# Strassen-Winograd products for the first value group of a SwiGLU layer, two of them placed before the second half's norm, and some sums of normed tiles on GpSimd

## The chip, the cores and the metric

One core of one Trainium2 chip. The metric is the device time of one execution in microseconds. Three timed runs of the kernel before gave a median of 2363.04 us (2362.53 to 2363.37).

## The reference

A two-layer trunk on a sequence of 1024 tokens, model width 1024, float32. Layer 0 mixes tokens with softmax attention with a forgetting gate, layer 1 with gated linear attention; each mixer is followed by a SwiGLU feed-forward of hidden width 2816. What matters here is the second half of each layer:

```python
h = modulate(rms_norm(x, norm2_g[i]), sh2, sc2)
x = x + g2[:, None, :] * swiglu(h, ffn_w_in[i], ffn_w_out[i])

def swiglu(h, w_in, w_out):
    gate, up = jnp.split(h @ w_in, 2, axis=-1)
    return (jax.nn.silu(gate) * up) @ w_out
```

## The kernel before, in words

**Number format.** Every float32 operand of a matmul is split into a high part (a cast on ScalarE) and a low part (a subtraction on VectorE or GpSimd), and a product is three matmuls: high by high, high by low, low by high (`mm3`, L305 to L307). Activations are kept transposed, so that a tile is 128 features by 512 tokens. `split_t` (L1516 and L1517 without a shift, L1519 and L1520 with one) splits a tile of activations, `split` (L174, L175) a block of weights.

**Two by two blocks.** The input product of the feed-forward is cut in two by two blocks. The normed input h has four blocks of four tiles each: B11 and B21 hold the first 512 tokens (features 0 to 511 and 512 to 1023), B12 and B22 the second 512. The weights come in groups of 256 output columns: group 0 of the gate, group 0 of the values, group 1 of the gate, and so on (`GROUPS`). A group has four weight blocks A11, A12, A21, A22 (first index: which 128 output columns; second: which 512 features) and four results C11, C12, C21, C22 (columns by token halves).

**Two ways to compute a group.** From the third group on, the loop `for X in gs[2:]` uses the Strassen-Winograd scheme: seven products of a block of four tiles, 12 matmuls each, instead of eight. The sums of weights (`op_sums`, L918 to L920, and `make_s4`, L930) are on GpSimd; the sums of activations are T1 = B12 - B11, T2 = B22 - T1, T3 = B22 - B12 and T4 = B21 - T2, made once per layer and kept as split tiles. The results are put together by additions on VectorE from PSUM (`add`, L1637). The first two groups, gate 0 and value 0, are computed by `plain_tile` instead: eight tiles of 24 matmuls, each over all eight tiles of one half of the tokens. A gate tile ends in a SiLU on ScalarE (L1667), a value tile in a multiplication on VectorE from PSUM (L1669).

**The stage that is changed.** The norm of the first half of the tokens comes early. The gate tiles (0, 0, 0) and (0, 1, 0), written as kind, column block, token half, run on it, and into the second of them are placed the sums over the partitions, the root (L714, L715) and the broadcast of the second half's norm (`rms_spread`, L727, into a PSUM tile called rb). Then `second_half` makes the second half: `normed` (L1512) multiplies the input with rb, `split_t` gives B12 and B22, and for each k the first sum is subtracted on GpSimd (L1701) and split into T1, and the second on VectorE (L1703) and split into T2. The six other plain tiles follow: value (1, 0, 0) on the first half, gate (0, 0, 1) and (0, 1, 1) on the second, and values (1, 0, 1), (1, 1, 1), (1, 1, 0). T3 (L1713) and T4 (L1718) are made behind them. T3 lies in the memory of B12 and T4 in that of the normed tiles y12 and y22, so they wait until those have been read.

**What sets the order.** The program's text gives the dependencies; a planner of the framework decides at compile time, from estimated durations, in which order each engine gets its instructions, and where an instruction of higher priority would not be ready it takes another one that is. At run time every engine works through its list in order. `tc.issue_after(ins)` and `behind_all()` add an order without a wait: the instructions of the block stand behind a given one on their engine. Weight blocks come through `feed.next()`, which keeps `feed.depth` of them in flight; the split blocks go through a ring of six slots, the raw ones through a ring of six views, and the DMA of a raw block is issued when its view has been read. `pin` is a ring of PSUM banks, eight of them in this stage. `tick()` in `prod` lets stores of finished hidden tiles go out after a number of products.

Of the kernel before, what the change touches and what calls it, by code (L numbers as in the profile page):

```python
# [53 lines left out]
def trunk(ctx, tc, x, c, ada_w, ada_b, norm1_g, norm2_g, ffn_w_in, ffn_w_out,  # L54
# [200 lines left out]
    @contextmanager  # L255
    def behind_all():

        bb = nc.cur_bb.bb.instructions
        n = len(bb)
        yield  # L260
        for i in bb[n:]:
            for e, at in split_after.items():
                if i.engine == ENG[e]:
                    tc.add_manual_dep(i, at.name, mybir.DependencyInfo(
                        mybir.DependencyClass.NoSync, mybir.DependencyReason.DATA), reason="order")
# [170 lines left out]
    def last_of(e):  # L436
        return next(i for i in reversed(nc.cur_bb.bb.instructions) if i.engine == ENG[e])
# [321 lines left out]
    class SumSq:  # L759
# [9 lines left out]
        def sums(self, psr, upto=None):  # L769

            if not self.done:
                self.sp = psr([P, self.n], F32, "sp")
            upto = len(self.roots) if upto is None else upto
            for i in range(self.done, upto):
                for t in range(self.n):
                    nc.tensor.matmul(self.sp[:, t:t + 1], self.roots[i][:, psl(t)], ones, start=i == 0 and t == 0,
                                     stop=i == len(self.roots) - 1 and t == self.n - 1)
                if i < len(self.roots) - 1:
                    self.ahead = last_ins()
            self.done = upto  # L780
# [122 lines left out]
    def op_block(l, gr, ab, *after):  # L903

        t = op_tile([depth(gr), P], f"o{l}{gr[0]}{gr[1]}{ab[0]}{ab[-1]}")
        split(t[:, 0], t[:, 1], raws[gr][ab])
        for a in after:
            op_raw(l, *a)
        return as_pair(t)
# [17 lines left out]
    def make_s4(gr):  # L927

        r = raws[gr]
        nc.gpsimd.tensor_sub(r[A12], r[A12], r[A11])  # L930
# [8 lines left out]
    def op_a12(l, gr):  # L939
        w = op_block(l, gr, A12)  # L940
        make_s4(gr)
        return w

    def op_out(l, k0, kc, m0, i):
        mw = 512 // kc
        raw = raw_view(0).rearrange("p (k m) -> p k m", k=kc)
        nc.sync.dma_start(raw, ffn_w_out[l, psl(k0, kc), m0:m0 + mw].rearrange("(k p) m -> p k m", p=P))
        t = op_tile([kc, mw], f"oo{l}{k0}{m0}")
        nc.scalar.copy(t[:, 0], raw)
        (nc.gpsimd if i == 2 else nc.vector).tensor_sub(t[:, 1], raw, t[:, 0].bitcast(F32))  # L950
        return as_pair(t)
# [59 lines left out]
    def ffn_loads(l):  # L1011

        blk = lambda gr, ab, *after: (op_block, l, gr, ab, *after)
        sums = lambda gr, *after: (op_sums, l, gr, *after)
        outs = lambda k0, kc, n: [(op_out, l, k0, kc, m0, i) for i in range(n) for m0 in range(0, D, 512 // kc)]
        g, u = GROUPS[:2]
        four = (A11, A21, A22, A12)
        r = [(op_first, l, g, A11, (g, four), (u, (A11, A12))), blk(g, A12), blk(g, A21), blk(g, A22, (u, (A21, A22)))]
        gs = GROUPS[1:] + OGROUPS
        for a, n in zip(gs, gs[1:] + [None]):  # L1020
            first, then = ((n, four[:2]),), ((n, four[2:]),)
            if n is None:
                first = then = ()
            if a == u:
                r += [blk(a, A11), blk(a, A12, *first), blk(a, A21), blk(a, A22, *then)]
                continue
            r += [blk(a, A11), sums(a, *first)]
            if a[0] < 2:
                r += [blk(a, A11), (op_a12, l, a), blk(a, A21, *then), blk(a, A22), blk(a, A12)]
            else:  # L1030
                r += [(op_s2, l, a), blk(a, A21, *then), blk(a, A12), blk(a, A22), blk(a, "s")]
        return r + outs(NFH - 4, 4, 2 + l)
# [440 lines left out]
    def ffn(l, oh, xs, slots, nm, mid, norm_end, each=None, blocks=None):  # L1473
# [40 lines left out]
        def split_t(t, y, shift=None):  # L1514
            if shift is None:
                nc.scalar.copy(hi(t), y)  # L1516
                nc.vector.tensor_sub(lo(t), y, hi(t).bitcast(F32))  # L1517
            else:
                nc.scalar.activation(hi(t), y, AF.Identity, bias=shift)  # L1519
                nc.vector.scalar_tensor_tensor(lo(t), y, shift, hi(t).bitcast(F32), op0=ALU.add, op1=ALU.subtract)  # L1520
# [24 lines left out]
        def gate_view(i, key):  # L1545

            if i % 2:
                return xs[key[0]][:, hsl(key[1])]
            if key[0] not in sgt:
                sgt[key[0]] = Views(sg[key[0]:key[0] + 1], 2, [HALF], f"sg{l}{key[0]}").v  # L1550
            return sgt[key[0]][key[1]]
# [33 lines left out]
        def hid_done(i, key):  # L1585

            v = {nm_: gate_view(i, k_) for k_, nm_ in BN.items()}
            nm_ = BN[key]
            if (nm_, i) in hid_d:
                defer(1, lambda: hid_out(nm_, i, v[nm_]))  # L1590
            got[i] = got.get(i, 0) + 1
            if i >= NST or got[i] < 4:
                return

            def t13():
                nc.gpsimd.tensor_sub(v["B11"], v["B12"], v["B11"])
                nc.gpsimd.tensor_sub(v["B12"], v["B22"], v["B12"])
                hid_out("T3", i, v["B12"])

            def t2():  # L1600
                hid_out("T1", i, v["B11"])
                nc.gpsimd.tensor_sub(v["B22"], v["B22"], v["B11"])

            def t4():
                hid_out("T2", i, v["B22"])
                nc.gpsimd.tensor_sub(v["B21"], v["B22"], v["B21"])
                hid_out("T4", i, v["B21"])
            defer(2, t13)
            defer(3, t2)
            defer(4, t4)  # L1610
# [36 lines left out]
        def plain_tile(kind, m, hf, after=(), steps=()):  # L1647
            wg = wgs[kind]
            ps = pin([P, HALF], F32, f"p{l}")
            for k in range(8):  # L1650
                if wg[m][k // 4] is None:
                    wg[m][k // 4] = feed.next()
                    feed.depth = 1
                w = wg[m][k // 4]
                t = (b["B12"] + b["B22"])[k] if hf else (B11 + B21)[k]
                with ExitStack() as es:
                    for ins in after:
                        es.enter_context(tc.issue_after(ins))
                    mm3(ps, w.hi[:, k % 4, :], w.lo[:, k % 4, :], hi(t), lo(t), k == 0, k == 7)
                if k in dict(steps):  # L1660
                    at = last_ins()
                    with tc.issue_after(at):
                        dict(steps)[k]()
                    after = (last_of("P"),)
            d = gate_view(0, (m, hf))
            if kind == 0:
                nc.scalar.activation(d, ps, AF.Silu)  # L1667
                return
            nc.vector.tensor_mul(d, d, ps)  # L1669
            hid_done(0, (m, hf))  # L1670

        def spread():
            r1.append(rms_spread(r1[0], f"{l}11", psr))
# [15 lines left out]
        def second_half(rb):  # L1689
            y = y12 + y22  # L1690
            lows = []
            for k in range(8 + 6):
                if k < 8:
                    with tc.issue_after(lows[k - 6]) if k >= 6 else ExitStack():
                        normed(y[k], k, 1, rb)
                k -= 6 - 1
                if 0 <= k < 8:
                    split_t((B12 + B22)[k], y[k], sh(k))
                    lows.append(last_of("D"))
            for k in range(4):  # L1700
                nc.gpsimd.tensor_sub(y11[k], y12[k], y11[k])  # L1701
                split_t(T1[k], y11[k])
                nc.vector.tensor_sub(y11[k], y22[k], y11[k])  # L1703
                split_t(T2[k], y11[k], sh(k + 4))

        second_half(r1[1])
        pin.q.extend(psr.q)
        for kind, m, hf in ((1, 0, 0), (0, 0, 1), (0, 1, 1), (1, 0, 1), (1, 1, 1), (1, 1, 0)):
            plain_tile(kind, m, hf, () if m or hf else (rb_ins[-1],))
        block("T3", H_SL[4:8])  # L1710
        T3 = b["T3"]
        for k in range(4):
            nc.vector.tensor_sub(y12[k], y22[k], y12[k])  # L1713
            split_t(T3[k], y12[k], ds[:, k:k + 1])
        block("T4", slots["to"])
        T4 = b["T4"]
        for k in range(4):
            nc.vector.tensor_sub(y21[k], y21[k], y11[k])  # L1718
            split_t(T4[k], y21[k])
        mid()  # L1720
        bk = list(pin.q)
        pin, pj = Ring(psp, bk[:5]), Ring(psp, bk[5:])
# [200 lines left out]
    def mid(*js):  # L1923
        v = Views(slots["hid"], 2, [HALF], f"ad{js[0]}").v
        ada1_queue(js, v[0][:, 0:256], v[1:4])
        ada1.at -= 20.0
# [553 lines left out]
```

## Time and profile before

| | |
|---|---|
| Median of three runs | 2363.04 us |
| The profiled execution | 2362.25 us |
| Its span, first to last instruction | 2360.5 us |
| Mean granted TensorE clock | 0.994 |
| TensorE busy | 2339.7 us (99%) |
| VectorE busy | 1791.0 us (76%) |
| ScalarE busy | 1122.5 us (48%) |
| GpSimd busy | 1101.5 us (47%) |

All views are of one profiled execution. In a timeline the first number of a row is the start in microseconds from the span's start, the second how long the row's instructions took from the first start to the last end, then engine, line, operation, output and inputs by name, and how many instructions were merged ("x4"). In brackets stands how long the engine was idle before the row and what ended that. PE is TensorE, DVE VectorE, ACT ScalarE, POOL GpSimd, SP the engine that issues the DMAs. The reported duration of one instruction overlaps with the next one's, so that the cost of one in a row of many is read from start to start.

### The profile page before, as it was taken

The page shows a single profiled execution, that of the slowest core. Times are in us where ns is not written, and L with a number is a line of the kernel's source. Part 1 is how long each engine was busy: PE and PEld are TensorE (multiplying, and loading weights), DVE is VectorE, ACT ScalarE, POOL GpSimd, SP SyncE. Part 2 cuts the span into 40 slices and gives each one's busy share as a digit, 9 for nine tenths or more (in the row PEclk, how much of TensorE's full clock was granted, in tenths as well). Part 3 has the DMA queues.
Part 4 walks back from the last instruction along what each step waited for, and adds up shares of the span by engine and source line. Part 5 has one row for each costly group of instructions (what it writes and reads, how often), then busy time and mean ns, then how long its engine had stood idle before and what let it go on. Part 6 is the DMA issues. An engine that isn't in the chain of part 4 may idle for free. (4 is left out here: it accounts for less than half of the span.)

```text
span 2360.5 us, 35758 instructions
## 1 busy us (share of the span) xinstructions
PE 2339.7 (99%) x12208; PEld 1992.7 (84%) x12208; DVE 1791.0 (76%) x2996; ACT 1122.5 (48%) x2186; POOL 1101.5 (47%) x993
## 2 busy tenths in 40 slices
PE   8999999999999999999999999999999999999999
PEld 7888888888888888888888898898888888888888
DVE  6578787886688888885788765668787777876787
ACT  6556566575453343345324644444453433345326
POOL 1334444533355666653363531345446665643262
PEclk8999999999999999999999999999999999999999
DMA  8423333332435545457665543554434544457664
GB/s 265 145 79 113 105 121 95 121 126 99 134 100 173 189 161 170 159 185 259 225 224 170 147 130 93 148 180 169 143 114 163 165 152 147 157 197 259 227 198 150
DMA packets 348719, 375.00 MB, mean 159 GB/s; under 512 B 25500, under 2 KB 286776, under 8 KB 348536
## 3 DMA queue, kind: packets, MB, share of 16 engines
q1 hardware_dynamic: 348536, 372.72, 48.2%
q8 instruction: 96, 1.57, 0.3%
q14 instruction: 87, 0.71, 0.1%
HBM read 275.56 MB, written 97.06 MB: 158 GB/s over the span
## 5 line engine op out<-in xcount | busy, mean ns | idle before, releaser
L175 DVE TENSOR_TENSOR o_s<-xv_s,o_s 128x512 fp32r<-128x512 f32 (+1 forms) x376 | 322.4, 862 | 54.5 <-ACT o_s L174 52.9
L174 ACT CAST o_s<-xv_s 128x512 fp32r<-128x512 f32 (+1 forms) x376 | 216.9, 587 | 290.5 <-PE p_b L307 239.1
L307 PE MATMUL p_b<-B,o_s 128*128 128x512 f32 x608 | 236.0, 389 | 0.0
L305 PE MATMUL p_b<-B,o_s 128*128 128x512 f32 x608 | 235.6, 390 | 0.4 <-DVE x L1637 0.4
L306 PE MATMUL p_b<-B,o_s 128*128 128x512 f32 x608 | 235.9, 389 | 0.0
L918 POOL TENSOR_TENSOR ex_s<-xv_s,xv_s 128x512 f32<-128x512 f32 (+1 forms) x64 | 90.5, 1414 | 285.1 <-DMA xv_s<-in_ffn_w_in_dram 118.8
L1272 POOL TENSOR_SCALAR lp_s<-lp_s,st 128x128 f32<-128x128 f32 (+7 forms) x128 | 98.1, 770 | 246.3 <-DVE st L1271 230.7
L305 PE MATMUL p_b<-T,o_s 128*128 128x512 f32 x480 | 186.9, 389 | 0.0
L306 PE MATMUL p_b<-T,o_s 128*128 128x512 f32 x480 | 186.8, 389 | 0.0
L307 PE MATMUL p_b<-T,o_s 128*128 128x512 f32 x480 | 181.2, 389 | 0.0
L305 PEld LDWEIGHTS p_b<-B,o_s 128*128 128x128 f32 x608 | 114.1, 188 | 24.5 <-DVE x L1637 1.0
L307 PEld LDWEIGHTS p_b<-B,o_s 128*128 128x128 f32 x608 | 114.1, 188 | 23.9
L306 PEld LDWEIGHTS p_b<-B,o_s 128*128 128x128 f32 x608 | 114.1, 188 | 23.5
L1270 ACT ACTIVATE lp_s<-lp_s,st 128x128 f32<-128x128 f32 (+7 forms) x128 | 99.4, 777 | 59.7 <-DVE st L1266 58.6
L920 POOL TENSOR_TENSOR xv_s<-ex_s,xv_s 128x512 f32<-128x512 f32 (+1 forms) x64 | 87.4, 1366 | 62.3 <-DVE o_s L175 60.0
L174 ACT CAST pt_s<-t_b 128x512 fp32r<-128x512 f32 (+1 forms) x160 | 79.7, 547 | 72.0 <-PE t_b L1292 71.4
L1637 DVE TENSOR_TENSOR ex_s<-ex_s,p_b 128x512 f32<-128x512 f32 x140 | 93.7, 681 | 19.6 <-PE p_b L307 19.5
L175 DVE TENSOR_TENSOR pt_s<-t_b,pt_s 128x512 fp32r<-128x512 f32 (+1 forms) x160 | 96.3, 630 | 15.7 <-ACT pt_s L174 15.1
L307 PEld LDWEIGHTS p_b<-T,o_s 128*128 128x128 f32 x480 | 90.1, 188 | 18.7
L305 PEld LDWEIGHTS p_b<-T,o_s 128*128 128x128 f32 x480 | 90.1, 188 | 18.6
L306 PEld LDWEIGHTS p_b<-T,o_s 128*128 128x128 f32 x480 | 90.1, 188 | 18.6
L246 POOL TENSOR_TENSOR w_l_s<-w__s,w_h_s 128x256 fp32r<-128x256 f32 x90 | 69.6, 801 | 76.7 <-ACT w_h_s L242 58.8
(1801 smaller groups left out, 7440.8 us busy)
## 6 DMA issues: line engine op xcount, KB each, us to landing
xv_s<-in_ffn_w_in_dram SPq DMA_DIRECT2D x176, 256.0 KB, 3.2
hid_B<-x SPq DMA_DIRECT2D x70, 512.0 KB, 2.9
ad_s<-in_ada_w_dram SPq DMA_DIRECT2D x384, 64.0 KB, 2.4
hid_T<-x SPq DMA_DIRECT2D x36, 512.0 KB, 2.9
xv_s<-in_ffn_w_out_dram SPq DMA_DIRECT2D x96, 192.0 KB, 5.0
ada_s<-in_ada_w_dram SPq DMA_DIRECT2D x96, 128.0 KB, 2.8
xv_s<-in_ffn_w_out_dram SPq DMA_DIRECT2D x40, 256.0 KB, 2.9
T2o<-hid_T SPq DMA_DIRECT2D x18, 512.0 KB, 8.5
```

The costliest lines, as they stand in the source:

```text
L174: nc.scalar.copy(hi, src)
L175: nc.vector.tensor_sub(lo, src, hi.bitcast(F32))
L246: (nc.gpsimd if i < 3 else nc.vector).tensor_sub(lo[:, cs], rw[:, cs], hi[:, cs].bitcast(F32))
L305: nc.tensor.matmul(ps, ah, bh, start=start, stop=False, skip_group_check=chain)
L306: nc.tensor.matmul(ps, ah, bl, start=False, stop=False, skip_group_check=chain)
L307: nc.tensor.matmul(ps, al, bh, start=False, stop=stop, skip_group_check=chain)
L918: nc.gpsimd.tensor_add(s1, a21, a22)
L920: nc.gpsimd.tensor_sub(a11, s1, a11)
L1270: nc.scalar.activation(lp, lp, AF.Exp, bias=mcur, scale=-1.0, accum_out=st[:, qi, 2:3])
L1272: nc.gpsimd.tensor_scalar(lp, lp, st[:, qi, 3:4], 1.0, op0=ALU.mult, op1=ALU.mult)
L1637: nc.vector.tensor_add(d, d if src is None else dest(G, src), ps)
```

## The change

In both layers the first value group (`u` in `ffn_loads`, `X = gs[1]` in `ffn`) is computed by the seven products in place of four plain tiles. Two of them, A11 by B11 and A12 by B21, need only the first half of the tokens; they stand in the program directly behind the broadcast of the second half's norm, then come the two gate tiles of the second half, and then the other five products in the order T1, T2, B22, T3, T4. The weights of the group go through `op_sums` and the new `op_s4`. The second sum (T2) moves from VectorE to GpSimd, and so do two of the four subtractions of T3 and two of the four of T4. The split of T1 is put behind the last low part of B12 and B22, the work of T3 behind the last low part of T2.

```diff
+    def op_s4(l, gr):
+        make_s4(gr)
+        return op_block(l, gr, A12)
...
             if a == u:
-                r += [blk(a, A11), blk(a, A12, *first), blk(a, A21), blk(a, A22, *then)]
+                r += [blk(a, A11), blk(a, A12), sums(a, *first), blk(a, A11), (op_s4, l, a), blk(a, A21, *then),
+                      blk(a, A22)]
                 continue
...
-            d = gate_view(0, (m, hf))
-            if kind == 0:
-                nc.scalar.activation(d, ps, AF.Silu)
-                return
-            nc.vector.tensor_mul(d, d, ps)
-            hid_done(0, (m, hf))
+            nc.scalar.activation(gate_view(0, (m, hf)), ps, AF.Silu)
...
+            split_after.update(D=last_of("D"))
             for k in range(4):
                 nc.gpsimd.tensor_sub(y11[k], y12[k], y11[k])
-                split_t(T1[k], y11[k])
-                nc.vector.tensor_sub(y11[k], y22[k], y11[k])
+                with behind_all():
+                    split_t(T1[k], y11[k])
+                nc.gpsimd.tensor_sub(y11[k], y22[k], y11[k])
                 split_t(T2[k], y11[k], sh(k + 4))
-
-        second_half(r1[1])
+            low2 = last_of("D")
+            split_after.clear()
+            return low2
+
+        low2 = second_half(r1[1])
         pin.q.extend(psr.q)
-        for kind, m, hf in ((1, 0, 0), (0, 0, 1), (0, 1, 1), (1, 0, 1), (1, 1, 1), (1, 1, 0)):
-            plain_tile(kind, m, hf, () if m or hf else (rb_ins[-1],))
+        X = gs[1]
+        with tc.issue_after(rb_ins[-1]):
+            nc.scalar.copy(dest(X, C11), prod(feed.next(), B11))
+            p2 = prod(feed.next(), B21)
+        for m in range(2):
+            plain_tile(0, m, 1)
+        feed.depth = 3
         block("T3", H_SL[4:8])
         T3 = b["T3"]
+        split_after.update(D=low2)
         for k in range(4):
-            nc.vector.tensor_sub(y12[k], y22[k], y12[k])
-            split_t(T3[k], y12[k], ds[:, k:k + 1])
+            with behind_all():
+                (nc.vector if k % 2 else nc.gpsimd).tensor_sub(y12[k], y22[k], y12[k])
+                split_t(T3[k], y12[k], ds[:, k:k + 1])
+        split_after.clear()
         block("T4", slots["to"])
         T4 = b["T4"]
         for k in range(4):
-            nc.vector.tensor_sub(y21[k], y21[k], y11[k])
+            (nc.vector if k % 2 else nc.gpsimd).tensor_sub(y21[k], y21[k], y11[k])
             split_t(T4[k], y21[k])
+        p5 = prod(feed.next(), T1)
+        add(X, C12, prod(feed.next(), T2), C11)
+        add(X, C11, p2)
+        fin(X, C11)
+        p3 = prod(feed.next(), B22)
+        add(X, C22, prod(feed.next(), T3), C12)
+        add(X, C12, p5)
+        add(X, C12, p3)
+        fin(X, C12)
+        add(X, C21, prod(feed.next(), T4), C22)
+        fin(X, C21)
+        add(X, C22, p5)
+        fin(X, C22)
```

## The prediction

> **What bounds the kernel now.** I read the page first, then who waits for whom on TensorE, then the timelines of TensorE, VectorE and GpSimd around the second half's norm in layer 0, then the same stretch of layer 1.
>
> ```profile
> span 2360.5 us, 35758 instructions
> ...
> PE 2339.7 (99%) x12208; PEld 1992.7 (84%) x12208; DVE 1791.0 (76%) x2996; ACT 1122.5 (48%) x2186; POOL 1101.5 (47%) x993
> ```
>
> TensorE is busy 99% of the span, so a matmul that is left out is worth its full pitch, as long as the operands of those left come in time. The pitch comes from one plain tile of 24 matmuls, (0, 0, 0), and the start of the stage from the row behind the broadcast:
>
> ```profile
> 644.25 0.61 PE L305 MATMUL p_b<-B,o_s 128*128 128x512 f32 x2
> ...
> 649.69 0.61 PE L305 MATMUL p_b<-B,o_s 128*128 128x512 f32 x2
> ...
> 656.98 1.05 PE L727 MATMUL rb_b<-ident,rs 128*128 128x128 f32 x8
> 657.79 0.47 PE L305 MATMUL p_b<-B,o_s 128*128 128x512 f32 x1
> ```
>
> From 644.25 to 649.69 is 5.44 us for 24 matmuls, 0.2267 us each; a block product of 12 is 2.72 us. The broadcast (L727) ends the wait for the norm, and at 657.79 the first matmul behind it starts. Six plain tiles from there, 32.64 us, end at 690.43, where the third group begins.
>
> VectorE in the same stretch:
>
> ```profile
> 658.08 4.04 DVE L1512 SCALAR_TENSOR_TENSOR yb_s<-x,amul,rb_b 128x512 f32<-128x512 f32 x6 [2.92 <-PE rb_b L727]
> 662.03 1.30 DVE L1520 SCALAR_TENSOR_TENSOR B<-yb_s,modc,B 128x512 fp32r<-128x512 f32 x1
> ...
> 672.55 0.68 DVE L1517 TENSOR_TENSOR T<-ya_s,T 128x512 fp32r<-128x512 f32 x1
> ...
> 678.63 0.68 DVE L1703 TENSOR_TENSOR ya_s<-yb_s,ya_s 128x512 f32<-128x512 f32 x1
> 679.23 0.68 DVE L1718 TENSOR_TENSOR ya_s<-ya_s,ya_s 128x512 f32<-128x512 f32 x1
> 679.84 1.78 DVE L1520 SCALAR_TENSOR_TENSOR T<-ya_s,modc,T 128x512 fp32r<-128x512 f32 x1
> ...
> 682.14 0.74 DVE L1520 SCALAR_TENSOR_TENSOR T<-ya_s,modc,T 128x512 fp32r<-128x512 f32 x1
> 682.80 0.68 DVE L1718 TENSOR_TENSOR ya_s<-ya_s,ya_s 128x512 f32<-128x512 f32 x1
> ...
> 684.67 0.74 DVE L1520 SCALAR_TENSOR_TENSOR T<-ya_s,modc,T 128x512 fp32r<-128x512 f32 x1
> ...
> 692.34 1.40 DVE L1520 SCALAR_TENSOR_TENSOR T<-yb_s,ds,T 128x512 fp32r<-128x512 f32 x2
> ...
> 696.67 0.68 DVE L1517 TENSOR_TENSOR T<-ya_s,T 128x512 fp32r<-128x512 f32 x1
> ...
> 700.88 0.67 DVE L1637 TENSOR_TENSOR x<-x,p_b 128x512 f32<-128x512 f32 x1
> ```
>
> VectorE has no idle gap from 658.08 to past 697. The last low part of T1 comes at 672.55, of T2 at 684.67, of T3 at 692.34 (two), of T4 at 696.67. In the third group T1 is wanted at 693.2, T2 at 695.9, T3 at 701.3, T4 at 704.0 (690.43 plus one, two, four and five products), so each has 6.7 us or more in hand. Layer 1 runs the same order at the same pace (38.53 us from the first row to the last of T4, against 38.59):
>
> ```profile
> 1713.65 4.04 DVE L1512 SCALAR_TENSOR_TENSOR yb_s<-x,amul,rb_b 128x512 f32<-128x512 f32 x6 [3.74 <-PE rb_b L727]
> ...
> 1752.18 0.68 DVE L1517 TENSOR_TENSOR T<-ya_s,T 128x512 fp32r<-128x512 f32 x1
> ```
>
> GpSimd over the same time:
>
> ```profile
> 658.97 5.53 POOL L1701 TENSOR_TENSOR ya_s<-yb_s,ya_s 128x512 f32<-128x512 f32 x4 [2.71 <-DVE yb_s L1512]
> 678.85 2.22 POOL L920 TENSOR_TENSOR xv_s<-ex_s,xv_s 128x512 f32<-128x512 f32 x1 [14.36 <-DVE o_s L175]
> 686.09 3.47 POOL L1596 TENSOR_TENSOR sg_s<-sg_s 128x512 f32<-128x512 f32 x1 [5.02 <-DVE sg_s L1669]
> 689.53 1.74 POOL L930 TENSOR_TENSOR xv_s<-xv_s,xv_s 128x512 f32<-128x512 f32 x1
> ...
> 694.72 3.79 POOL L918 TENSOR_TENSOR ex_s<-xv_s,xv_s 128x512 f32<-128x512 f32 x1 [3.46 <-DMA xv_s<-in_ffn_w_in_dram]
> 698.59 3.52 POOL L919 TENSOR_TENSOR xv_s<-xv_s 128x512 f32<-128x512 f32 x1
> ```
>
> **One resource under two engines.** The rows show that a GpSimd sum and a VectorE instruction with two inputs from SBUF don't run at once. L920 starts at 678.85 while VectorE does plain subtractions until 679.84; it ends at 681.07, 1.23 us behind them, and the VectorE instruction that starts at 679.84 takes 1.78 instead of the 0.66 that the rows 682.14 and 682.80 show from start to start. L919 waits through a row of subtractions until 700.88, where VectorE takes an input from PSUM, and ends at 702.11, again 1.23 later. So I count 0.60 us for a subtraction (678.63 to 679.23), 0.66 for a low part with a shift, and 1.24 for a GpSimd sum, all from one account. Test it on the kernel before, from 662.03 to the end of T4:
>
> ```profile
> L1520 DVE SCALAR_TENSOR_TENSOR B<-yb_s,modc,B 128x512 fp32r<-128x512 f32 x8 | 6.8, 859 | 0.0
> L1517 DVE TENSOR_TENSOR T<-ya_s,T 128x512 fp32r<-128x512 f32 x8 | 5.4, 680 | 0.0
> L1520 DVE SCALAR_TENSOR_TENSOR T<-yb_s,ds,T 128x512 fp32r<-128x512 f32 x4 | 4.9, 1256 | 0.0
> L175 DVE TENSOR_TENSOR o_s<-xv_s,o_s 128x512 fp32r<-128x512 f32 x7 | 4.7, 679 | 0.0
> L1520 DVE SCALAR_TENSOR_TENSOR T<-ya_s,modc,T 128x512 fp32r<-128x512 f32 x4 | 4.0, 1000 | 0.0
> L1517 DVE TENSOR_TENSOR x<-sg_s,x 128x512 fp32r<-128x512 f32 x2 | 1.4, 678 | 0.0
> L175 DVE TENSOR_TENSOR o001s_s<-ex_s,o001s_s 128x512 fp32r<-128x512 f32 x1 | 0.7, 678 | 0.0
> ```
>
> Sixteen with a shift (8 + 4 + 4) are 10.6 us. Of plain ones there are 8 for T1 and T4, 12 subtractions for T2, T3 and T4 (four each in the loops), 8 weights and 2 hidden tiles, 30 in all, 18.0 us. GpSimd has 1.8 of the four sums at 658.97 left and three more by 691.27, 5.9 us. Sum 34.5, so 696.5; the trace has 697.3. The account holds to 0.8 us.
>
> **The change part by part.**
>
> *Matmuls.* Four value tiles are 96 matmuls, seven products 84. Twelve less per layer, 2.72 us, over two layers 5.44 us less.
>
> *When operands are wanted.* From 657.79: two products on the first half (5.44), two gate tiles (10.88), so T1 is wanted at 674.11, T2 at 676.83, B22 at 679.55, T3 at 682.27, T4 at 684.99, and its last low part about ten matmuls later, at 687.26. That is 19 us earlier than before for T1 to T4. B12 and B22 themselves are in time: eight low parts from 662.03 (5.3) with what is left of T1's GpSimd sums (2.2, below) end at 669.5, T1's own four (2.4) at 671.9, ahead of 674.11.
>
> *What has to be done by then.* With a shift: sixteen as before, 10.6. Plain: 8 for T1 and T4, 4 subtractions left on VectorE, and five weight blocks (the sum, A11 again, the sum of `op_s4`, A21, A22), 17 in all, 10.2. GpSimd: 1.8 sums of T1 (2.2), and now 4 for T2, 2 for T3, 2 for T4, 9.9. Sum 32.9 us, so T4 is complete at 662.03 + 32.9 = 694.9, where TensorE wants it at 687.3: **7.6 us late**. The eight moved subtractions are 4.8 us of the account on VectorE and 9.9 on GpSimd, so on this account the move costs 5.1 us per layer where it is meant to relieve VectorE. Additions from PSUM (up to five ahead of T4) and the last two normed tiles, 0.6 to 0.67 us each, lie beside the 12.1 us of GpSimd and cost nothing while that lasts; without this cover they would add 4.3 us.
>
> [...] If the engines were independent, VectorE alone would be through with T4 near 686, and the stage would have no stall.
>
> *What hides it.* The planner fills holes that it foresees. In the kernel before it did that a great deal: gate tile (0, 0, 1), which in the text's order would be done at 668.7, had its SiLU at 679.97, and (0, 1, 1) at 681.63, with the other tiles' matmuls taken between.
>
> ```profile
> 679.97 0.58 ACT L1667 ACTIVATE sg_s<-p_b 128x512 f32<-128x512 f32 x1
> ...
> 681.63 0.59 ACT L1667 ACTIVATE sg_s<-p_b 128x512 f32<-128x512 f32 x1
> ```
>
> Behind the changed group there are matmuls of the next one that need no T4: A11 by B11, T1 and T2, 8.16 us. Their banks come free only once T2's product has been added. Whether they are put ahead is decided on the planner's durations, and VectorE's own instructions (8 normed tiles 5.4, then 10.6 + 10.2, and five additions 3.0) would end near 687.3 without GpSimd in the way, about when T4 is wanted. So it will see little of the delay. Bounds for what it pulls ahead: nothing (stall 7.6) and all 8.16 us (stall none, below which nothing can go, since the matmuls are the floor). I take 1.36 us, half a product, nearest to the single matmuls that are out of order in such stretches. Stall 6.2 us per layer.
>
> *GpSimd and the root.* In layer 1 two sums of weights for the third group stand in front of the root, and TensorE waits:
>
> ```profile
> 1708.78 1.27 POOL L918 TENSOR_TENSOR ex_s<-xv_s,xv_s 128x512 f32<-128x512 f32 x1 [13.05 <-DMA xv_s<-in_ffn_w_in_dram]
> 1710.13 1.30 POOL L919 TENSOR_TENSOR xv_s<-xv_s 128x512 f32<-128x512 f32 x1
> 1711.39 1.02 POOL L715 TENSOR_TENSOR rs<-rs,mhalf 128x4 f32<-128x4 f32 x1
> ```
>
> ```profile
> PE rb_b L727 <- POOL rs L715: 0.6, 1, 0.6
> ```
>
> After the change the third group's last raw blocks are loaded later (their views hold the value group's blocks until its second A11 and `op_s4` are split), so these sums can't come there, and the value group's own find GpSimd idle for 13 us before 1708.78. I take the 0.55 us as won; the bounds are 0.55 won and 1.3 lost, one sum in front of the root. ScalarE gets three more casts of weights and one copy per layer; at 48% busy over the span it has room for them. The late raw blocks land about 3 us after issue
>
> ```profile
> xv_s<-in_ffn_w_in_dram SPq DMA_DIRECT2D x176, 256.0 KB, 3.2
> ```
>
> and are summed and split by 688 or so, ahead of 690.4, where the third group wants its sum; the stall gives them more time. On SP's queue they only change places with stores.
>
> *Sum.* Against the span: 2360.5 - 5.44 - 0.55 + 2 x 6.2 = 2366.9. The profiled execution took 2362.25, 1.75 more than its span, and the median of the runs is 0.79 above that: 2369.4 us, 0.27% slower. (About 0.2%, 4.7 us, is what a measurement of this kernel can tell from no change.)
>
> **The rivals.**
>
> *The order hides it (chance 0.28).* The planner puts up to three products of the third group ahead of T3 and T4, or the additions, sums and low parts fit closer than the account allows, and the stall is 0 to 1 us: 2363.0 - 6.0 + 0 to 2 = 2357.0 to 2359.0. For it: the 8.16 us of other work are there, TensorE shows no stall in this stretch before, and the planner reordered it. Against it: on VectorE's own times T4 seems punctual. It decides from about 6.6 us pulled ahead.
>
> *One whole product ahead (0.20).* Stall 7.6 - 2.72 = 4.9: 2363.0 - 6.0 + 9.8 = 2366.8, within 0.2%.
>
> *More on GpSimd in front of T4's sums (0.10).* Two sums of weights of the third group and the multiplication that ends C11 get in line before them, 3.7 us more: stall 11.3, 2363.0 - 6.0 + 22.6 = 2379.6.
>
> *My case (0.42).* Stall from 5.3 to 8.4 us per layer (the account's 0.8 added above), 2367.6 to 2373.8.
>
> **How the numbers follow.** Faster by over 0.2%, below 2358.3: most of the first rival, 0.23. Within 0.2%: its rest, the second rival and a little of mine, 0.28. Slower: 0.49. Range 2357.0 to 2374.0, which leaves out the third rival and a margin of my own case, under 2 in 10 together.
>
> **What would show it.** In the changed profile: 24 matmuls fewer. TensorE waiting for low parts of T2, T3 or T4 (L1517, L1520, or the GpSimd sums behind them), 5 to 8 us in each layer between about 677 and 696, and the same after 1732. GpSimd sums of normed tiles of over 1.3 us beside rows of VectorE subtractions, and T4's last low part near 695. The root of layer 1 without its wait. I am wrong if TensorE runs through this stretch without a gap: then either the third group's products lie ahead of T4's, or T4's low parts come by 688 and the account is wrong. The gain in matmuls is wrong if the stage's TensorE time doesn't shrink by 2.7 us per layer.

## The result, and the profile after

| | median of the runs | lowest to highest | runs |
|---|---|---|---|
| before | 2363.83 us | 2362.53 to 2365.68 | 6 |
| after | 2402.20 us | 2400.12 to 2408.88 | 6 |

The changed kernel is 38.4 us slower: ratio 1.0167, 95% interval 1.0152 to 1.0183. The profiled execution took 2400.25 us. The direction was forecast, the size was not: 2369.4 us were expected, 6.4 us above the 2363.04 known then, and the range ended at 2374.0.

The page of the changed kernel:

```profile
span 2398.5 us, 35767 instructions
...
PE 2350.0 (98%) x12184; PEld 1991.6 (83%) x12184; DVE 1837.9 (77%) x2992; ACT 1130.7 (47%) x2194; POOL 1149.8 (48%) x1025
```

TensorE has 24 matmuls fewer than before, as counted, and is nevertheless busy 10.3 us longer (2350.0 against 2339.7). So the loss can't be waits alone: some matmuls must have become slower.

Where the loss arises can be read from the start of matmuls that both kernels have (us in the profiled execution):

| first matmul of | before | after | behind by | added since the row above |
|---|---|---|---|---|
| `fo1471`, the last tile ahead of the stage, layer 0 | 641.53 | 641.29 | -0.24 | |
| `f0e018`, the first tile of `hh` by `oo`, the tail of the layer | 1245.23 | 1262.72 | 17.49 | 17.7 |
| `f0e11801`, eight tiles on | 1267.08 | 1286.92 | 19.84 | 2.35 |
| `od`, in the mixer of layer 1 | 1675.37 | 1697.44 | 22.07 | 2.2 |
| `f1e018`, the tail of layer 1 | 2300.10 | 2336.52 | 36.42 | 14.35 |
| `ft`, behind it | 2321.96 | 2360.39 | 38.43 | 2.0 |

The two stages hold 32 us of the 38, the two tails 4.3. Within the stage of layer 0 the view of who waits for whom on TensorE, from 640 to 740, has these groups (total us, times, longest); in the kernel before this stretch has no wait:

```profile
PE p_b L307 <- DVE o_s L175: 2.1, 1, 2.1
PE p_b L307 <- DVE o001s_s L175: 1.9, 1, 1.9
PE sp_b L776 <- DVE ss_s L792: 1.8, 1, 1.8
PE p_b L306 <- DVE T L1525: 1.1, 2, 0.7
PE p_b L305 <- DVE x L1642: 0.9, 1, 0.9
PE p_b L305 <- ACT o_s L174: 0.8, 1, 0.8
PE p_b L306 <- DVE B L1525: 0.7, 1, 0.7
PE p_b L305 <- ACT T L1524: 0.4, 1, 0.4
```

They add up to 9.7 us; in layer 1 the same view gives 11.6. Only 1.5 us of the 9.7 are put down to the split T tiles; the two longest waits, and 4.8 us in all, are for split blocks of weights (`o_s`, `o001s_s`), whose low parts VectorE makes as well. The third row is the norm's: the ones-matmul L776 waits for the sums of squares. The second row is for weights of the third group of products (`o001s`), which the planner had put ahead of T4.

The other part is the clock. The view by stretches of 3.41 us gives the length of the stretch, TensorE's busy time and matmuls in it, its granted clock, and the DMA:

```profile
652.36:655.77 3.41, 1.65 (x11) 1.00 0.77 308
655.77:659.19 3.42, 3.42 (x14) 0.50 0.00 0
659.19:662.60 3.41, 3.41 (x13) 0.50 0.02 5
...
686.49:689.90 3.41, 1.28 (x6) 1.00 0.06 19
689.90:693.31 3.41, 2.73 (x7) 0.50 0.69 201
693.31:696.73 3.42, 2.62 (x7) 0.50 0.35 97
696.73:700.14 3.41, 1.47 (x3) 0.50 0.26 68
700.14:703.55 3.41, 3.41 (x10) 0.50 0.02 5
...
724.04:727.45 3.41, 1.68 (x7) 1.00 0.57 182
727.45:730.86 3.41, 3.41 (x9) 0.50 1.01 327
```

Seven of these stretches are at 0.50. TensorE was busy for 20.5 us in them, so 10.2 us of that is lost to the clock. In the timeline a matmul of the slow stretch follows the one before it after 0.42 us, where the pitch is otherwise 0.2267:

```profile
657.91 0.63 PE L306 MATMUL p_b<-B,o_s 128*128 128x512 f32 x1
658.33 0.63 PE L307 MATMUL p_b<-B,o_s 128*128 128x512 f32 x1
```

Layer 0 then adds up: 9.7 of waits and 10.2 of half clock, less the 2.72 of matmuls left out, is 17.2, against 17.7 from the starts. Layer 1 has three slow stretches (from 1734.38, 1765.10 and 1775.34), 5.1 us: 11.6 + 5.1 - 2.72 - 0.55 (the old wait for the root, which is gone) = 13.4, against 14.35.

Why the norm is late shows in GpSimd's and VectorE's timelines ahead of it. GpSimd first:

```profile
639.67 1.49 POOL L918 TENSOR_TENSOR ex_s<-xv_s 128x512 f32<-128x512 f32 x1 [4.63 <-DMA xv_s<-in_ffn_w_in_dram]
641.24 1.62 POOL L919 TENSOR_TENSOR xv_s<-xv_s,xv_s 128x512 f32<-128x512 f32 x1
647.47 1.61 POOL L920 TENSOR_TENSOR xv_s<-ex_s,xv_s 128x512 f32<-128x512 f32 x1 [4.61 <-DVE o_s L175]
649.16 1.62 POOL L930 TENSOR_TENSOR xv_s<-xv_s 128x512 f32<-128x512 f32 x1
```

These are the value group's own sums of weights, beside VectorE's low parts of the first half (L1525) and a residual addition (L1415):

```profile
639.92 1.78 DVE L1525 SCALAR_TENSOR_TENSOR B<-ya_s,modc,B 128x512 fp32r<-128x512 f32 x1
...
647.85 3.48 DVE L1525 SCALAR_TENSOR_TENSOR B<-ya_s,modc,B 128x512 fp32r<-128x512 f32 x2
651.25 0.74 DVE L1415 SCALAR_TENSOR_TENSOR x<-fo1461p_b,modc,x 128x512 f32<-128x512 f32 x1
```

A low part takes 1.78 us instead of 0.66, two take 3.48, and the residual addition starts at 651.25, where before it was 647.91. The sums of squares stand behind it, TensorE waits 1.79 us for them, two slow stretches follow, and the second half's first normed tile starts at 663.02 instead of 658.08.

The second stage on GpSimd, from T2's sums on:

```profile
677.94 6.98 POOL L1705 TENSOR_TENSOR ya_s<-yb_s,ya_s 128x512 f32<-128x512 f32 x3 [4.55 <-DVE T L1522]
...
691.90 1.70 POOL L918 TENSOR_TENSOR ex_s<-xv_s,xv_s 128x512 f32<-128x512 f32 x1 [1.91 <-DVE ya_s L1731]
693.68 1.60 POOL L919 TENSOR_TENSOR xv_s<-xv_s 128x512 f32<-128x512 f32 x1
695.36 1.60 POOL L920 TENSOR_TENSOR xv_s<-ex_s,xv_s 128x512 f32<-128x512 f32 x1
698.85 1.61 POOL L930 TENSOR_TENSOR xv_s<-xv_s,xv_s 128x512 f32<-128x512 f32 x1 [1.89 <-issue]
```

and on VectorE:

```profile
666.98 1.24 DVE L1525 SCALAR_TENSOR_TENSOR B<-yb_s,modc,B 128x512 fp32r<-128x512 f32 x1
...
682.75 1.01 DVE L1525 SCALAR_TENSOR_TENSOR T<-ya_s,modc,T 128x512 fp32r<-128x512 f32 x1 [1.94 <-ACT T L1524]
683.69 1.78 DVE L1731 TENSOR_TENSOR ya_s<-ya_s,ya_s 128x512 f32<-128x512 f32 x1
...
705.79 0.68 DVE L1522 TENSOR_TENSOR T<-ya_s,T 128x512 fp32r<-128x512 f32 x1
```

From the first low part, 666.98, to the end of T4's last, 706.39, are 39.4 us; the account gave 32.9. The four sums of the third group (L918 to L930, 691.90 to 700.46) got in ahead of T4's low parts, at 1.24 us each 5.0 us, and VectorE made the low parts of ten weight blocks in this time, where the account had five, another 3.0 us. With both the account comes to 40.9 us, 1.5 more than the trace has: its prices hold roughly, but work was missing from its list. VectorE was idle for 1.94 us at 682.75, while GpSimd did sums for T2, which the account has in GpSimd's part.

### The profile page after: what moved, and what is told of

Its sections match the earlier page's. It is cut to its first block, busy times and chain, and to the rows that moved or that the text cites. A ratio compares the mean times of both kernels' runs of the same rounds, so it can differ in the third digit from the quotient of the medians.

```text
span 2398.5 us, 35767 instructions
## 1 busy us (share of the span) xinstructions
PE 2350.0 (98%) x12184; PEld 1991.6 (83%) x12184; DVE 1837.9 (77%) x2992; ACT 1130.7 (47%) x2194; POOL 1149.8 (48%) x1025
## 5 line engine op out<-in xcount | busy, mean ns | idle before, releaser
L175 DVE TENSOR_TENSOR o_s<-xv_s,o_s 128x512 fp32r<-128x512 f32 (+1 forms) x380 | 328.7, 869 | 44.1 <-ACT o_s L174 43.4
L306 PE MATMUL p_b<-B,o_s 128*128 128x512 f32 x568 | 222.7, 393 | 1.4 <-DVE B L1525 1.3
L305 PE MATMUL p_b<-B,o_s 128*128 128x512 f32 x568 | 221.6, 393 | 0.0
L307 PE MATMUL p_b<-B,o_s 128*128 128x512 f32 x568 | 217.5, 392 | 0.0
L918 POOL TENSOR_TENSOR ex_s<-xv_s,xv_s 128x512 f32<-128x512 f32 (+1 forms) x64 | 88.2, 1378 | 257.7 <-DMA xv_s<-in_ffn_w_in_dram 81.1
L305 PE MATMUL p_b<-T,o_s 128*128 128x512 f32 x504 | 197.5, 393 | 3.6 <-ACT o_s L174 2.0
L306 PE MATMUL p_b<-T,o_s 128*128 128x512 f32 x504 | 197.6, 393 | 2.1 <-DVE T L1525 2.1
L307 PE MATMUL p_b<-T,o_s 128*128 128x512 f32 x504 | 191.9, 392 | 4.3 <-DVE o_s L175 4.3
L306 PEld LDWEIGHTS p_b<-B,o_s 128*128 128x128 f32 x568 | 107.4, 189 | 25.2 <-DVE B L1525 3.1
L307 PEld LDWEIGHTS p_b<-B,o_s 128*128 128x128 f32 x568 | 107.5, 189 | 22.4
L305 PEld LDWEIGHTS p_b<-B,o_s 128*128 128x128 f32 x568 | 107.3, 189 | 22.3
L1642 DVE TENSOR_TENSOR ex_s<-ex_s,p_b 128x512 f32<-128x512 f32 x154 | 104.4, 680 | 27.5 <-PE p_b L307 27.4
L305 PEld LDWEIGHTS p_b<-T,o_s 128*128 128x128 f32 x504 | 95.2, 189 | 25.3 <-ACT o_s L174 2.9
L307 PEld LDWEIGHTS p_b<-T,o_s 128*128 128x128 f32 x504 | 95.3, 189 | 24.6 <-DVE o_s L175 5.1
L306 PEld LDWEIGHTS p_b<-T,o_s 128*128 128x128 f32 x504 | 95.1, 189 | 24.7 <-DVE T L1525 5.3
L930 POOL TENSOR_TENSOR xv_s<-xv_s,xv_s 128x512 f32<-128x512 f32 x40 | 54.3, 1356 | 116.5 <-issue 83.8
```

What stands on the lines that cost most here:

```text
L175: nc.vector.tensor_sub(lo, src, hi.bitcast(F32))
L305: nc.tensor.matmul(ps, ah, bh, start=start, stop=False, skip_group_check=chain)
L306: nc.tensor.matmul(ps, ah, bl, start=False, stop=False, skip_group_check=chain)
L307: nc.tensor.matmul(ps, al, bh, start=False, stop=stop, skip_group_check=chain)
L918: nc.gpsimd.tensor_add(s1, a21, a22)
L1642: nc.vector.tensor_add(d, d if src is None else dest(G, src), ps)
```

## The experiments

Each kernel ran between runs of the kernel before on the same chip, whose median was 2362.3 to 2364.8; the ratios are against those. "After" below is the 2402.2 us above. The three kernels with two runs each have intervals that reach into that of the changed kernel (1.0152 to 1.0183), so the single gains read from them are rough; which waits went is seen in their profiles.

| kernel | median, us | runs | ratio, 95% interval |
|---|---|---|---|
| after, sums of normed tiles on VectorE | 2390.84 | 2 | 1.0115 (1.0067 to 1.0163) |
| before, moved sums alone | 2371.84 | 8 | 1.0033 (1.0018 to 1.0048) |
| after, value group's weight sums behind the root | 2396.22 | 2 | 1.0138 (1.0107 to 1.0168) |
| after, no forced order on VectorE | 2396.43 | 2 | 1.0139 (1.0108 to 1.0169) |
| before, root later by two powers | 2366.01 | 10 | 1.0011 (1.0001 to 1.0021) |
| before, root later by four | 2375.44 | 4 | 1.0052 (1.0037 to 1.0067) |
| before, root later by eight | 2381.89 | 4 | 1.0083 (1.0066 to 1.0100) |
| after, banks turned back | 2402.89 | 4 | 1.0174 (1.0157 to 1.0190) |
| after, three repairs | 2385.28 | 4 | 1.0094 (1.0079 to 1.0109) |
| the same, next group's sums behind T4 | 2378.91 | 4 | 1.0061 (1.0044 to 1.0078) |
| the same, two more products ahead | 2378.35 | 4 | 1.0063 (1.0048 to 1.0078) |

**The moved sums, taken back and alone.** The changed kernel with the eight moved subtractions per layer on VectorE again, and the kernel before with nothing but the move:

```
-                nc.gpsimd.tensor_sub(y11[k], y22[k], y11[k])
+                nc.vector.tensor_sub(y11[k], y22[k], y11[k])
...
-                (nc.vector if k % 2 else nc.gpsimd).tensor_sub(y12[k], y22[k], y12[k])
+                nc.vector.tensor_sub(y12[k], y22[k], y12[k])
...
-            (nc.vector if k % 2 else nc.gpsimd).tensor_sub(y21[k], y21[k], y11[k])
+            nc.vector.tensor_sub(y21[k], y21[k], y11[k])
```

> The changed kernel with all twelve second, third and fourth sums of normed tiles (T2, T3, T4) back on VectorE. Theory A (the shared account of VectorE and GpSimd, and a TensorE clock that halves after each gap): eight sums fewer at 1.24 us and eight more at 0.60 us, 5 us per layer off the account; TensorE's waits for T1 to T4 behind 684 us fall from 6.2 to about 2 us in layer 0 and the half-speed stretch behind them shrinks from 13 to about 5 us; the gap in front of the norm's sums over partitions (L776, 1.8 and 2.3 us) stays. Total about 2386 us. Rival B (the seven products ask for T2 to T4 too early, whichever engine makes them): the waits only change places, total within 5 us of 2402. Rival C (the order forced on VectorE is to blame): also within 5 us of 2402.

> The kernel before, with only the moves of sums to GpSimd (all four of T2, two each of T3 and T4); the value group stays on plain tiles and no order is forced. Theory A: T4 comes some 5 us later than before, inside the 6.7 us it has in hand, so TensorE shows no gap and the time is within 3 us of 2363.8. Rival B: the same. If the moves alone are the cause of the loss, it is over 2375.

Taking the move back gains 11.4 us (its two runs lie 7.7 us apart), about what the account asks for the two layers (10.2), but not in the way that theory A has it. The four waits from 686 to 694 us in layer 0 still come to 5.0 us, and not to 2. In the profiled execution the waits of both layers come to 15.7 us in place of 21.3, and TensorE was busy for 21.2 us in slow stretches there, 10.6 us lost in place of 15.3: nearly half of what that execution saves in the two stages is the clock. Alone the move costs 7 to 8 us: TensorE, where each T had 6.7 us or more in hand, now waits four times in each layer, 0.35, 0.42, 2.00 and 0.41 us. In that profile the clock is 1.00 in both stages (0.999 over the execution) and its time is 2365.27, but the eight runs reach up to 2376.89. No theory had these waits. So the move is a loss in either order of work; after it is undone, 27 us of the 38 remain.

**The value group's weight sums, put behind the norm.**

```
+        with tc.issue_after(root_ins["G"]) if gr == GROUPS[1] else ExitStack():
             nc.gpsimd.tensor_add(s1, a21, a22)
             nc.gpsimd.tensor_sub(a21, a11, a21)
             nc.gpsimd.tensor_sub(a11, s1, a11)
```

> The changed kernel with the value group's three sums of weights (L918 to L920, and with them the fourth, L930) ordered behind the root of the second half's norm on GpSimd; before that nothing of theirs is beside the residual additions and sums of squares on VectorE. Theory A: the gap in front of L776 (1.8 and 2.3 us) and its half-speed stretch (about 3 us) go, in both layers, but the four sums (5 us) come into the later account; total between 2390 and 2402, the gap at L776 under 0.3 us. Rival B: the gap at L776 has another cause and stays.

The wait at L776 is gone in both layers, and so is the slow clock behind it, as theory A has it: from 645.57 to 686.53 in layer 0 and from 1713.94 to 1761.73 in layer 1 the clock is 1.00. The kernel gains 6.0 us. A new wait of 1.71 us for a low part of B12 or B22 (L1526) takes part of the gain back, since the sums now collide with those low parts.

**The order forced on VectorE, taken away.**

```
-                with behind_all():
-                    split_t(T1[k], y11[k])
+                split_t(T1[k], y11[k])
...
-            with behind_all():
-                (nc.vector if k % 2 else nc.gpsimd).tensor_sub(y12[k], y22[k], y12[k])
-                split_t(T3[k], y12[k], ds[:, k:k + 1])
+            (nc.vector if k % 2 else nc.gpsimd).tensor_sub(y12[k], y22[k], y12[k])
+            split_t(T3[k], y12[k], ds[:, k:k + 1])
```

> The changed kernel without the order that it forces on VectorE (T1's split behind the last low part of B12 and B22, T3's work behind T2's last low part). Rival C: the planner's own order is better, total under 2390. Theory A: the account is the same and so is the end of T4 within 2 us; T1 or T3 are taken ahead of B12 and B22 or T2, which TensorE waits for first; total 2400 to 2412.

It gains 5.8 us: the forced order seems to cost more than it brings here, and theory A's 2400 to 2412 is missed, but the theory that it is the main loss (below 2390) falls. A wait of 2.32 us for low parts of B12 and B22 appears earlier, and the waits for T2 to T4 become shorter.

**What a wait of TensorE costs.** In the kernel before, GpSimd raises the root to the power 1 two, four or eight times more, which delays the norm and nothing else (`mone` is a tile of ones):

```
         nc.gpsimd.tensor_tensor(rs, rs, mhalf[:, 0:n], op=ALU.pow)
+        for _ in range(2 if nm[1:] == "11" else 0):
+            nc.gpsimd.tensor_tensor(rs, rs, mone[:, 0:n], op=ALU.pow)
```

> The kernel before with two more GpSimd powers (exponent 1) of about 1.0 us each behind the second half's root in both layers, nothing else: it opens one wait of TensorE per layer, of about 1.3 us in layer 0 (no wait was there, and the root is some 0.7 us early) and 2.6 us in layer 1 (0.55 was there). Theory A (a wait of about 2 us or more is followed by some us in which the granted clock is near 0.5, and costs them too): 2370 to 2375, with slow 4-us windows behind the wait of layer 1. Rival B (a wait costs its own length): 1.3 and 2.05 us more, 2367 to 2369, clock 1.00 behind both.

> The same with four more powers: waits of about 3.4 us in layer 0 and 4.65 us in layer 1, 7.5 us together beyond the 0.55 that was there. Theory A: half clock behind both, 5 to 14 us more than the waits, 2377 to 2386. Rival B: 2371 to 2374. The difference to the run with two powers tells how the price grows with the length of one wait.

> The kernel before with eight more powers behind the second half's root: waits of about 7.3 us in layer 0 and 8.5 us in layer 1, 15.3 us together beyond the 0.55 that was there. Theory G (the granted clock is set anew every 3.41 us, on a grid that runs through the whole execution, by how idle the stretch before was, so that what a wait costs beyond its length is one or two half-speed stretches, however long it is): half speed for at most 3.41 + 3.41 us behind each wait, ends of the slow stretches a whole number of 3.413 us apart between the two layers, 2380 to 2384. Rival L (the slow stretch grows with the wait: in the run with four powers it was about as long as the wait): 2386 to 2392.

With two, the waits are 1.33 us in layer 0 and 2.34 in layer 1. The row of the second, and the clock around it:

```profile
1717.30 1.16 PE L731 MATMUL rb_b<-ident,rs 128*128 128x128 f32 x8 [2.34 <-POOL rs L719]
```

```profile
1712.00:1716.00 4.00, 2.96 (x16) 1.00 0.06 18
1716.00:1720.00 4.00, 2.70 (x16) 1.00 0.00 0
```

That is 3.1 us beyond the 0.55 of before, and the time went up by 2.8. Here a wait cost its own length, as the rival has it (its 2367 was 1 us too much), and behind a wait of 2.34 us the clock stayed at 1.00. With four the waits are 1.94 (and 0.52 for the sums of squares) and 4.00, 5.9 us more; the time went up by 12.3. Layer 1's clock in stretches of 3.41 us:

```profile
1721.84:1725.25 3.41, 0.27 (x2) 1.00 0.00 0
1725.25:1728.66 3.41, 3.41 (x13) 0.50 0.00 0
1728.66:1732.08 3.42, 3.42 (x16) 1.00 0.00 0
```

In layer 0 two stretches are slow, 656.88 to 660.29 and 663.70 to 667.12; the first lies before the wait for the root, behind the norm's small matmuls. The three slow stretches cost 5.1 us, and with the waits that makes 11.0. Against both forecasts (2371 to 2374 and 2377 to 2386) 2375.44 lies between, so neither theory fits. What the profiles of every kernel with slow stretches show is that their starts and ends are whole multiples of 3.413 us apart, also from one layer to the other: in the changed kernel from 655.77 to 1775.34 are 1119.57 us, 328 times 3.4133. With eight powers the waits are 7.85 and 8.48 us:

```profile
1724.22:1727.63 3.41, 0.00 (x0) 1.00 0.00 0
1727.63:1731.04 3.41, 0.00 (x0) 0.50 0.00 0
1731.04:1734.46 3.42, 3.40 (x12) 0.50 0.00 0
1734.46:1737.87 3.41, 3.41 (x16) 1.00 0.00 0
```

Only 5.25 us behind layer 0's wait and 3.4 behind layer 1's ran slow, and the time went up by 19.6: 15.8 of waits beyond the old one and 4.3 of half clock make 20.1. In layer 1 a wait of 8.48 us draws no longer slow stretch behind it than one of 4.00 did, and the time lies in the grid theory's range, not in the other's (2386 to 2392).

**The PSUM banks of the tail.** The stage takes nine tiles from the ring of banks where it took six, and the tail then begins with another bank:

```
         bk = list(pin.q)
+        bk = bk[5:] + bk[:5]
         pin, pj = Ring(psp, bk[:5]), Ring(psp, bk[5:])
```

> The changed kernel with the ring of PSUM banks turned back alone. Theory A (the stage now takes nine tiles from the ring instead of six, so that the tail's last chunk meets a bank that VectorE still holds): the waits of 1.56 and 1.30 us on the last chunk's products behind VectorE's L1879 vanish, 2396 to 2400. Rival D (VectorE is only late there, whatever the bank): the waits stay, 2400 to 2405.

The tail's product that waited, on TensorE, in the changed kernel and with the banks turned back:

```profile
1268.43 0.50 PE L305 MATMUL f0e01800p_b<-hh,oo_s 128*128 128x512 f32 x1 [1.56 <-DVE x L1879]
```

```profile
1264.53 0.47 PE L305 MATMUL f0e01800p_b<-hh,oo_s 128*128 128x512 f32 x1 [0.29 <-issue]
```

The waits vanish in both layers, and the tail's tiles are as quick as before (from `f0e018` to `f0e11801` 0.01 us are added, where it was 2.35). So theory A has the waits right, but 2402.89 us is in the rival's range. The time did not fall: in this profiled execution the two stages took 18.6 and 17.1 us more than in the kernel before, where the table above has 17.7 and 14.35, with six slow stretches in layer 1 instead of three. The cause of the waits is shown; whether the turn gains anything is not, since the slow stretches of one execution and another differ by as much.

**Three repairs together**, and then one more: the third group's weight sums held behind T4's low parts by a GpSimd copy that reads the last of them.

> The changed kernel with the sums of normed tiles back on VectorE, the value group's weight sums of this stage behind the second half's root, and the ring of PSUM banks turned back for the stage's tail. Theory A (three separate losses: about 11.4 us by the moved sums, 6.0 by the weight sums ahead of the norm, about 4 by the banks): 2379 to 2384, with waits of about 2 us for the T tiles left in both layers. Rival D (the first two are the same loss, seen twice, because weight sums put later meet the sums of tiles): 2386 to 2392. The new order paying by itself would show as below 2365.

```
-        with tc.issue_after(root_ins["G"]) if gr == GROUPS[1] else ExitStack():
+        at = root_ins["G"] if gr == GROUPS[1] else t4_read[l] if gr == GROUPS[2] else None
+        with tc.issue_after(at) if at else ExitStack():
...
             split_t(T4[k], y21[k])
+        nc.gpsimd.tensor_copy(t4_col, lo(T4[3])[:, 0:1].bitcast(F32))
+        t4_read[l] = last_of("G")
```

> The three repairs, and the third group's weight sums held behind T4's low parts by a small GpSimd copy that reads the last of them. Theory A (in the three repairs these sums run beside the sums for T3, which take 1.16 us instead of 0.62, and T3 and T4 are late by it): the sums for T3 take about 0.62, the last wait of 4.51 us for T4 falls to about 2.3, 2379 to 2383. Rival D (the third group's own products wait for its weights instead): a new wait of 2 us or more behind the third group's first product, 2384 to 2388.

The three repairs gain 16.9 us, of 17.4 that the first two gained singly: separate losses for the most part, as far as these rough single gains can tell, though the time lies just outside either range. In it VectorE does the four sums for T3 beside the third group's sums, and TensorE waits for a low part of T3 (L1526 adds a shift, so it is not T4, as the expectation has it):

```profile
685.75 4.64 DVE L1726 TENSOR_TENSOR yb_s<-yb_s,yb_s 128x512 f32<-128x512 f32 x4
```

```profile
693.34 0.79 PE L306 MATMUL p_b<-T,o_s 128*128 128x512 f32 x1 [4.51 <-DVE T L1526]
```

With these sums held back the same instructions and the wait are

```profile
684.25 2.48 DVE L1728 TENSOR_TENSOR yb_s<-yb_s,yb_s 128x512 f32<-128x512 f32 x4
```

```profile
688.65 0.50 PE L307 MATMUL p_b<-T,o_s 128*128 128x512 f32 x1 [2.42 <-DVE T L1528]
```

and the time falls by 6.4 us: about half the wait, and one slow stretch per layer where there were two and three. This is close to the prediction's third rival: GpSimd's sums of the next group get in, here in front of the low parts of T3 and T4 rather than of T4's sums.

**Two more products ahead.** The third group's A11 by B11 and A12 by B21 need no sum of tiles; here they, and the product with B22, come earlier (the order of the weights follows):

```
         p5 = prod(feed.next(), T1)
+        p3 = prod(feed.next(), B22)
         add(X, C12, prod(feed.next(), T2), C11)
         add(X, C11, p2)
         fin(X, C11)
-        p3 = prod(feed.next(), B22)
+        V = gs[2]
+        ps = prod(feed.next(), B11)
+        nc.scalar.copy(dest(V, C11), ps)
+        nc.scalar.copy(dest(V, C12), ps)
+        add(V, C11, prod(feed.next(), B21))
+        fin(V, C11)
         add(X, C22, prod(feed.next(), T3), C12)
```

> The same, with two products of the third group that need no sum of normed tiles (its A11 by B11 and A12 by B21) ahead of T3 and T4, and the product with B22 ahead of T2: 24 matmuls, 5.4 us, of further cover per layer. Theory A (the waits for the T tiles are the whole loss that is left, with the half-speed windows behind them): no wait over 0.9 us before T4, at most one half-speed window per layer; the kernel before less 5.4 us of matmuls, plus 1 to 2 us of waits and up to 1.7 us of half speed per layer, 2360 to 2366. Rival D (VectorE is behind for the whole stage, so that the waits only move into the third group's products): 2369 to 2380.

No gain over the last, and the rival's range. The waits on TensorE in layer 0:

```profile
684.48 0.50 PE L308 MATMUL p_b<-B,o_s 128*128 128x512 f32 x1 [1.07 <-DVE o_s L176]
690.13 0.50 PE L307 MATMUL p_b<-T,o_s 128*128 128x512 f32 x1 [2.57 <-DVE T L1528]
...
715.90 0.47 PE L306 MATMUL p_b<-B,o_s 128*128 128x512 f32 x1 [1.82 <-DVE x L1648]
```

The products in front wait for their weights' low parts (L176), T4's still come late (L1528, without a shift here), and the rest moves behind, to additions on VectorE (L1648). VectorE has no idle gap through T4's last low part; cover on TensorE moves its lateness, and doesn't shorten its work. No version beat the kernel before.

## Why the prediction was wrong

*Right.* 24 matmuls fewer; TensorE waiting for late split tiles in both layers, though for those of weights (4.8 and 5.5 us) more than for those of T (1.5 and 2.2), which alone were named; the move of sums as a loss (5.1 us per layer by the account, 5.7 by taking it back, the latter with the clock in it); the layer 1 root's wait gone.

*"The value group's own [weight sums] find GpSimd idle", cost nothing.* This step failed. GpSimd was idle, but VectorE was not, and by the prediction's own account a GpSimd sum and VectorE's work add up (a low part took 1.78 us beside a sum, 0.66 without). Four sums of 1.24 us stood beside the low parts and residual additions that the norm needs. Put behind the root they give back 6.0 us (two runs). The prediction looked for them in the one queue and not in the account that it had just set up. The root did lose its 0.55 us wait; the sums of squares took its place with 1.8 and 2.3.

*"Stall 6.2 us per layer", priced at its own length.* Two things were off. The waits were 9.7 and 11.6 us, 8.9 more over both layers: 4.1 of them the norm's, and T4 was later by the third group's four sums, much as in the rival that had 0.10, and by its weight blocks. And the half clock behind them, 10.2 + 5.1 = 15.3 us, had no term at all. This step failed too: a wait was priced at its own length, and the half clock that it left out is the largest single part of the error. The changed stage of the kernel before didn't show such a cost, as its one wait there is 0.55 us, but an earlier part of the same profile did. In the mixer of layer 0 TensorE waited 1.82 us for GpSimd, until 414.09, and the next stretch ran at half clock, 1.7 us of TensorE's time lost:

```profile
412.12:415.54 3.42, 1.60 (x11) 1.00 0.14 43
415.54:418.95 3.41, 3.41 (x15) 0.50 0.87 267
```

*What the planner pulls ahead, "I take 1.36 us".* The planner did more: B22's product came ahead of T2's, and products of the third group ahead of T4's. It helped little, as these waited for their own weights (`o001s`, 1.94 us), whose sums come from the same account.

*Not foreseen:* the tails, 4.3 us, by a ring of PSUM banks that the new number of tiles turns. The 2.2 us between the stages were not tried; 1.29 of them are one wait of TensorE in the mixer of layer 1 (`gr` behind VectorE's L2095) that the kernel before doesn't have, and its cause is open.

The forecast of 2369.4 was 32.8 us short of the median: 15.3 by the clock, 8.9 by longer waits, 4.3 in the tails and 2.2 between the stages are 30.7 of them.

## What to carry to other kernels

Where the work of two engines adds up, as here (two low parts took 3.48 us beside GpSimd sums, at 0.66 each without), the account has to run over everything that both do, also the work that goes to the "idle" one of them at another place. A GpSimd sum that stands beside VectorE's work costs here twice what the same sum costs on VectorE (1.24 against 0.60 us). And a wait of TensorE can cost more than its length: behind 1.82 us in the kernel before, a stretch of 3.41 us at half clock lost another 1.7 us. A change that trades a few matmuls for short waits needs its waits priced with that, and the profile before, read for slow stretches over its whole length, may already show the price.

## What the runs showed of the hardware

The tables by stretches of the two stages show this for the ten profiled kernels that have slow stretches there. Each stretch of 3.413 us is at 1.00 or at 0.50 throughout, and slow times are 3.41, 6.83, 10.24 or 13.65 us long. In one execution their starts and ends are whole multiples of 3.413 us apart; from one execution to another this grid lies elsewhere (a slow stretch starts at 655.77 us in the changed kernel, at 657.90 with the sums back on VectorE). Slow stretches went with how long TensorE was idle in the stretch before, rather than with the length of one wait. Of the stretches at full clock without the norm's small matmuls, all 21 in which TensorE was idle for 1.94 us or more were followed by a slow one, none of those with 1.58 or less, and four of seven between 1.62 and 1.74. With the norm's matmuls in them (128 by 1), stretches with less were followed by a slow one: 0.73 us idle in the changed kernel (from 1730.97), 0.52 with four powers (from 653.47), 0.39 with the banks turned back (from 654.71). Of the slow stretches, those with 0.66 us idle or more were each followed by another, and those with under 0.55 by none unless the norm's matmuls were in them. These are counts of the two stages, and at the head of an execution it was otherwise: in the kernel before 2.72 us idle in the stretch from 2.53 were followed by full clock.

How long one wait is does not tell it alone. The 1.82 us in the mixer of layer 0 of the kernel before lie in one stretch, and the next was slow. In the changed kernel the same wait takes 1.98 us, until 413.82, of which 1.58 lie in one stretch and 0.40 in the next, and the clock stayed at 1.00 (the stretches from 410.01, 413.42 and 416.83). With two powers it stayed at 1.00 behind a wait of 2.34 us; how that one lay on the grid is not shown. In slow stretches, 0.68 and 0.80 us idle (from 689.90 and 693.31 above) were followed by further slow ones. The spread of one program's runs, up to 11.6 us, goes with the clock: for the moved sums alone the mean granted clock falls from 0.999 in the run of 2365.27 us to 0.992 in that of 2376.89. Which stretches were slow there is not shown, as a profile shows a single execution.
